# Nine extra matmuls removed, nine weight products read and written in plain order: a decoder layer in split fp32 on one Trainium2 core

## The chip, the cores and the metric

The kernel runs on one NeuronCore of a Trainium2 chip. The metric is device time in microseconds, the median over repeated runs. Beside it stands one profiled execution with its span (first to last instruction) and a trace of every engine. TensorE does matrix products (the profile calls its matmuls PE and its weight loads PEld), VectorE is DVE, ScalarE is ACT, GpSimd is POOL, and SyncE (SP) issues most DMA transfers.

## The reference

One inference step of a one-layer hybrid decoder: a prompt of 256 tokens and 8 samples of 8 tokens share the same weights, so there are T = 320 token columns in all.

```python
xn = rms_norm(x, g_mix)
z = xn @ w_in              # split into b_gate, c_gate, h_conv, q, k, v, gate_c, gate_a
u = c_gate * h_conv
y_conv = (b_gate * short_conv(u, prev, w_conv)) @ w_conv_out
y_attn = window_attention(q, k, v, rel_bias, sinks) @ w_attn_out
merged = sigmoid(gate_c) * y_conv + sigmoid(gate_a) * y_attn
h = x + merged @ w_o
hn = rms_norm(h, g_ffn)
h = h + (silu(hn @ w_gate) * (hn @ w_up)) @ w_down
y = rms_norm(h, g_final)
```

The model width is 2048, the feed-forward width 5632. There are 16 query heads and 4 key/value heads of 64, with a window of 128 keys, a relative-position bias and a learned sink in the softmax. Also returned are the last keys, values and convolution rows of both groups.

## The kernel before, in words

**Features on partitions, tokens on columns.** An activation row is one tile row for 128 features, with 320 columns. A weight product takes a 128x128 block of weights as the stationary operand, streams one row of 320 columns past it and adds into a PSUM bank of 320 of 512 columns.

**Every value is kept as two fp32r parts,** a high part and the low rest. `split_to` (L128 to L130) makes the parts of a weight block: ScalarE copies the block to `whi`, VectorE subtracts that from the block into `wlo`. A product then takes three matmuls for each weight block: high weight by high row, high weight by low row, low weight by high row.

**Products.** `product` (L172) makes two banks of 128 output features over `nk` row chunks. It loads weights four chunks at a time (`load_cols`, 512 KB each through SyncE's queue) and goes through the matmuls in the order that `passes` gives: high and low row for a block at once, the low weight three blocks later. Its matmuls are all recorded on L186. The product of keys and values, `kv_product` (L346), is the same with four banks; its matmuls are on L372. With 16 chunks, a call of `product` is 96 matmuls.

**Plain order and turns.** A row of 320 columns lies in SBUF as five segments of 64 (`row_tiles`, L116): all chunks of segment 0 first, then all of segment 1, with 16 columns of padding after each. So one row is five runs of 64 neighbouring columns, 1,040 columns apart for 16 chunks. The bank is seen as five runs of 64 as well, but these lie one behind the other. `turns` (L101) rearranges such a view so that a matmul takes four columns of the first segment, four of the second and so on, then the next four of the first. Every weight product reads its row and writes its bank in turns. In plain order it would take all 64 columns of a segment before the next one; the bank would then be written from column 0 to 319.

```python
def turns(ap):
    return ap.rearrange("p s (i b) -> p i s b", b=4)
```

**The nudges.** `nudge` (L205 to L207) issues one extra matmul. It reads 320 neighbouring columns from the start of a row tile, uses 128 neighbouring columns of another row as its weights, and writes columns 0 to 319 of a spare PSUM bank that nobody reads. It is called at nine places: once in the product of keys and values before chunk 6 (L353), once before the third query product (L819), three times in the prompt's attention (after the last group of scores, L653, and after each of two groups of value products, L663), twice in the samples' attention (after the scores, L697, and after the value products, L768), and before the first product with `w_up` of each half of the feed-forward part (L1051).

**What sets the order.** The program is written in the order in which TensorE is to run it. The attention and other side work are Python generators. `tick` (L145) takes one step of the generator after every four chunks of a product, so groups of attention matmuls stand between the chunks of the products for q, C, H and B. `issue_after` marks keep the side work behind the last matmul and the last split. The stages run in this order: keys and values; q; C, H and B with attention beside them; the gates with the two output projections (gc, ga, yc, ya); `w_o` (wo); then two halves of the feed-forward part, each with gate and up products in turn (fg, fu) and then the down product (dn).

**Down.** `down` (L974) reads and writes in turns too, with 512 columns per matmul on L997 and 320 on L1005. Two matmuls in each group of 18, on L1001 (dl), stream 512 neighbouring columns into a bank in plain order.

Of the kernel before, what the change touches and what calls it, by code (L numbers as in the profile page):

```python
# [17 lines left out]
T = TP + NB * TS  # L18
# [8 lines left out]
P = 128  # L27
# [25 lines left out]
def hybrid_layer(ctx: ExitStack, tc: tile.TileContext, a: dict, o: list):  # L53
    nc = tc.nc
# [17 lines left out]
    def ps_aux(name):  # L72
        return aux[0].tile([P, 512], F32, tag="aux", name=name)
# [3 lines left out]
    def u(s):  # L77
        uid[0] += 1
        return f"{s}_{uid[0]}"
# [21 lines left out]
    def turns(ap):  # L101

        return ap.rearrange("p s (i b) -> p i s b", b=4)

    def fives(ap):

        return ap.rearrange("p (s j) -> p s j", s=NS)
# [24 lines left out]
    def load_cols(w, k0, n, c0, behind=()):  # L132
# [4 lines left out]
            split_to(hi[:, :n, :], lo[:, :n, :], raw[:, :n, :])  # L137
        return hi, lo

    mark = {}  # L140
    side_work = [None]
    pending = []
    last = {}
# [28 lines left out]
    def product(load, nk, xh, xl, name, tiles=None, loaded=None):  # L172

        ps = [ps_acc(u(name)) for _ in range(2)]
        k0 = 0
        for n in tiles or [min(KT, nk - k) for k in range(0, nk, KT)]:
            hi, lo = load(k0, n)
            if loaded:
                loaded()
            order = [(k, c) for k in range(n) for c in range(2)]  # L180
            if k0 + n == nk:
                order.sort(key=lambda kc: kc[1])
            for k, c, i in passes(order, k0 + n == nk):
                kc = k0 + k
                w, x = ((hi, xh), (hi, xl), (lo, xh))[i]
                last["mm"] = nc.tensor.matmul(  # L186
                    turns(fives(ps[c][:, :T])), w[:, k, c * P:(c + 1) * P], turns(x(kc)),
                    start=(kc == 0 and i == 0), stop=(kc == nk - 1 and i == 2),
                )
            k0 += n  # L190
            while pending:
                with after(last["lo"], last["mm"]):
                    pending.pop(0)()
            tick()
        return ps

    def two_parts(src, tags=("ta", "tb")):
# [3 lines left out]
        nc.scalar.activation(hi, src, AF.Copy)  # L201
        nc.vector.tensor_sub(lo, src, hi.bitcast(F32))
        return hi, lo

    def nudge(rows, weights, n=T):  # L205
        x, w = (bass.AP(r.tensor, r.offset, [list(r.ap[0]), [1, m]]) for r, m in ((rows(0), n), (weights(0), P)))
        nc.tensor.matmul(ps_aux(u("nudge"))[:, :n], w, x, start=True, stop=True)  # L207

    def over_partitions(out, parts):
        for i, x in enumerate(parts):  # L210
# [48 lines left out]
    xh, xl = row_tiles(xp, ("xh_t", "xl_t"), KC, LEAD_X, ("xh", "xl"))  # L259
# [26 lines left out]
    def x_load(i, eng=nc.sync):  # L286
# [11 lines left out]
        out=ident, in_=ident, compare_op=ALU.not_equal, fill=1.0, base=0, pattern=[[-1, P]],  # L298
# [47 lines left out]
    def kv_product(tiles, x_after):  # L346

        ps = [ps_acc(u("kv")) for _ in range(4)]
        k0 = 0
        x_prep(0)  # L350
        for i, n in enumerate(tiles):
            if k0 == 6:
                nudge(xh, xl)  # L353
            hi, lo = load_kv(k0, n)
            if i == 0:
                x_prep(1)
            for b in x_after.get(i, ()):
                x_load(b)
            order = [(k, c) for k in range(n) for c in range(4)]
            if k0 + n == KC:  # L360
                order.sort(key=lambda kc: kc[1])
            seq = passes(order, k0 + n == KC)
            if i == 0:
                seq.sort(key=lambda kcm: kcm[2])
            for k, c, m in seq:
                kc = k0 + k
                if k0 and (k, c, m) == (0, 3 if n > 1 else 1, 0) and k0 + n < KC:
                    for kk in range(tiles[i + 1]):
                        x_prep(k0 + n + kk)
                    tick()  # L370
                w, x = ((hi, xh), (hi, xl), (lo, xh))[m]
                last["mm"] = nc.tensor.matmul(  # L372
                    turns(fives(ps[c][:, :T])), w[:, k, c * P:(c + 1) * P], turns(x(kc)),
                    start=(kc == 0 and m == 0), stop=(kc == KC - 1 and m == 2),
                )
            k0 += n
            if i == 0:
                tick()
        return ps
# [88 lines left out]
    def at_rows(part):  # L468
# [15 lines left out]
        out=sides[:, 0], in_=sides[:, 0], compare_op=ALU.is_ge, fill=0.0, base=-1, pattern=[[-1, WIN]],  # L484
# [158 lines left out]
    def prompt_attention():  # L643
        units = [(j * 2 + par, gp) for j in range(2) for gp in range(2) for par in range(2)]
        bias, sc, sm, turned, pts = {}, {}, {}, {}, {}
        bias[0] = bias_load(*units[0])
        for i in range(len(units) + 3):
            if i < len(units):
                if i + 1 < len(units):
                    bias[i + 1] = bias_load(*units[i + 1])  # L650
                sc[i] = prompt_scores(*units[i], bias.pop(i))
                if i + 1 == len(units):
                    nudge(xh, xl)  # L653
                yield
                sm[i] = prompt_softmax(*units[i], sc[i])
            if 0 <= i - 3 < len(units):
                pts[i - 3] = prompt_sides(i - 3, turned.pop(i - 3))
            yield
            if i >= 4 and i % 4 == 2:
                for n in (i - 5, i - 3):  # L660
                    kv, gp = units[n]
                    prompt_pv(kv // 2, gp, (pts.pop(n - 1), pts.pop(n)))
                nudge(xh, xl)  # L663
            if 0 <= i - 1 < len(units):
                turned[i - 1] = prompt_norm(i - 1, sc.pop(i - 1), *sm.pop(i - 1))
            yield
# [3 lines left out]
    def sample_attention(sm):  # L670
# [10 lines left out]
        for base in range(0, NB, 3):  # L681
            ps = ps_aux(u("pss"))
            n = min(3, NB - base)
            for b in range(base, base + n):
                o0 = (b - base) * W2
                for kv in range(NKV):
                    j, par = kv // 2, kv % 2
                    rows = slice(par * 64, par * 64 + 64)
                    nc.tensor.matmul(
                        ps[kv * 32:(kv + 1) * 32, o0:o0 + W2], qs[rows, j, b, :], kf[rows, b, j, :],  # L690
                        start=True, stop=True,
# [2 lines left out]
                s[:, base:base + n, :], ps[:, 0:n * W2].rearrange("p (b k) -> p b k", b=n),  # L694
                flip(bias_s).unsqueeze(1).to_broadcast([P, n, W2]),
            )
        nudge(xh, xl)  # L697
        yield
        yield

# [49 lines left out]
        for j in range(2):  # L750
            for par in range(2):
# [4 lines left out]
                    start=True, stop=False,  # L756
                )
        for b in range(NB):
            cv = cvs.pop(b)
            for j in range(2):  # L760
                for par in range(2):
# [3 lines left out]
                        cv[:, kv * HD:(kv + 1) * HD], ptw[:, kv, b * 32:(b + 1) * 32],  # L765
                        start=False, stop=(b == NB - 1),
                    )
        nudge(xh, xl)  # L768
        yield
        for j in range(2):  # L770
            src = pos[j][:, 0:256].rearrange("p (b g t) -> p g b t", b=NB, g=GRP)
            o = LEAD_A + j * 4 * at_row
            rows = at_t[:, o:o + 4 * at_row].rearrange("p (g w) -> p g w", g=GRP)[:, :, -2 * JS:]
# [42 lines left out]
    for j in range(2):  # L816
        for gp in range(2):
            if (j, gp) == (1, 0):
                nudge(xh, xl)  # L819
            ps = in_pair(O_Q + (j * 2 + gp) * CW, "q")  # L820
            pending.append(lambda j=j, gp=gp, ps=ps: q_out(j, gp, ps))
    side_work[0] = attention()
# [2 lines left out]
    for cp in range(4):  # L825
        c_sb = []
        ps = in_pair(O_C + cp * CW, "C")
# [4 lines left out]
        ps = in_pair(O_H + cp * CW, "H")  # L832
        conv = []
        for c in range(2):
# [13 lines left out]
            n = UL - 2  # L848
# [10 lines left out]
        ps = in_pair(O_B + cp * CW, "B")  # L859
# [17 lines left out]
    mm = mp_.enter_context(tc.tile_pool(name="mm", bufs=1, side="right"))  # L877
# [9 lines left out]
    for mp in range(8):  # L887
        c0 = mp * CW
        sg = {}
        for nm, off, tag in (("gc", O_GC, "ta"), ("ga", O_GA, "tb")):  # L890
            ps = in_pair(off + c0, nm)
# [5 lines left out]
        ps = product(  # L897
            lambda k0, n: load_cols(w_co, k0, n, c0), 8,
            cv_h, cv_l, "yc",
        )  # L900
# [126 lines left out]
    for half in range(2):  # L1027
# [4 lines left out]
        for fpair in range(nf // 2):  # L1032
            c0 = (f0 + fpair * 2) * P
            psg = product(
                lambda k0, n: load_cols(w_g, k0, n, c0), KC,
                hh, hl, "fg",
            )
            if half == 0 and fpair == 0:
                pss = ps_aux("pss2")
                over_partitions(pss[:, :T], two_parts(hacc, ("tc", "td")))  # L1040
                rstd_of(pss[:, :T], [P, T], "r2", hp, out=rb2)
            gs = []
            for c in range(2):
                t, t2 = tmp("ta", "gs")[:, :T], tmp("tb", "sg")[:, :T]
                nc.vector.tensor_mul(t, psg[c][:, :T], rb2)
                last["sig"] = nc.scalar.activation(t2, t, AF.Sigmoid)
                nc.vector.tensor_mul(t, t, t2)
                nc.vector.tensor_mul(t, t, rb2)
                gs.append(t)
            if fpair == 0:  # L1050
                nudge(hh, hl)  # L1051
            psu = product(
                lambda k0, n: load_cols(w_u, k0, n, c0), KC,
                hh, hl, "fu",
            )
            for c in range(2):
                nc.vector.tensor_mul(gs[c], psu[c][:, :T], gs[c])
                f = fpair * 2 + c
                (first, rest), row = parts_of(gs[c]), a_move(f)
                nc.scalar.activation(row[:, :, JR:JT], rest, AF.Copy)  # L1060
                last["hi"] = nc.scalar.activation(row[:, :, 0:JR], first, AF.Copy)
                nc.vector.tensor_sub(row[:, :, JT:], rest, row[:, :, JR:JT].bitcast(F32))
                last["lo"] = nc.vector.tensor_sub(placed(a_low(f)), first, row[:, :, 0:JR].bitcast(F32))
                if half == 1:
                    nc.scalar.activation(a_first(f), gs[c][:, 0:P], AF.Copy)
# [258 lines left out]
```

## Time and profile before

| | us |
|---|---|
| median of 3 runs (1593.12 to 1593.64) | 1593.38 |
| profiled execution | 1593.85 |
| its span | 1592.1 |
| PE busy | 1583.2 |
| weight loads busy (beside PE) | 1547.1 |
| DVE busy | 890.9 |
| ACT busy | 645.9 |

The profiled execution is 0.47 us over the median. Its span is 1.75 us short of its own time; that is what lies around the span. TensorE's clock was granted at 0.998 over the span. A matmul's row in the trace gives its start and its duration; the duration counts the way through the array as well (301 ns for 320 columns), and the next matmul starts before it has ended. What a matmul costs in a dense stream is thus the distance from its start to the next start, not the duration.

### The profile page before, as it was taken

How to read it: one execution, taken by the hardware profiler on the slowest of the kernel's cores; microseconds unless marked ns; L12 is line 12 of the kernel's file. 1: busy time of each engine (PE TensorE's matmuls, PEld its weight loads, DVE VectorE, ACT ScalarE, POOL GpSimd, SP SyncE). 2: the span in 40 equal slices, each digit the busy share in tenths (PEclk: the TensorE clock that was granted, in tenths of full speed). 3: DMA queues.
4: the chain of work that ended last, by engine and by line, in shares of the span. 5: the costliest groups of instructions: out<-in, count | busy, mean ns of one | idle time of the engine just before them, and what ended most of it. 6: DMA issues, size and time to landing. Idle time of an engine off the chain costs nothing.

```text
span 1592.1 us, 26453 instructions
## 1 busy us (share of the span) xinstructions
PE 1583.2 (99%) x10899; PEld 1547.1 (97%) x10899; DVE 890.9 (56%) x1314; ACT 645.9 (41%) x917; POOL 133.2 (8%) x213
## 2 busy tenths in 40 slices
PE   9999999999999999999999999999999999999998
PEld 9999999999999999999999999998888999999887
DVE  7879765445555445556555555553444455555556
ACT  7554443333333333344333333333333334444443
POOL 1414332000000003320000000000000000000021
PEclk9999999999999999999999999999999999999999
DMA  7757566544455544455554545555555454445663
GB/s 271 207 182 218 171 211 203 166 154 155 157 159 159 159 156 155 155 158 159 157 154 155 159 158 159 159 156 161 155 155 157 157 159 158 156 155 157 190 180 131
DMA packets 77648, 266.06 MB, mean 167 GB/s; under 512 B 9832, under 2 KB 13112, under 8 KB 77400
## 3 DMA queue, kind: packets, MB, share of 16 engines
q1 hardware_dynamic: 71736, 249.99, 50.2%
q0 software_dynamic: 5360, 13.84, 3.0%
q8 instruction: 85, 1.39, 0.4%
q10 hardware_dynamic: 432, 0.56, 0.1%
q14 instruction: 35, 0.29, 0.1%
HBM read 257.27 MB, written 9.04 MB: 167 GB/s over the span
## 4 chain that ended last, share of the span: by engine, by line
PE 99%; DMA 0%; DVE 0%; ACT 0%; issue 0%; SPq 0%; DVEq 0%
PE fu L186 19%; PE fg L186 19%; PE dn L997 9%; PE wo L186 7%; PE gc L186 7%; PE ga L186 7%; PE dn L1005 6%; PE C L186 3%; PE B L186 3%; PE H L186 3%; PE q L186 3%; PE ya L186 3%; PE yc L186 3%; PE dl L1001 2%; PE kv L372 2%; PE dn L1162 1%
## 5 line engine op out<-in xcount | busy, mean ns | idle before, releaser
L130 DVE TENSOR_TENSOR wlo<-wraw,whi 128x1024 fp32r<-128x1024 f32 (+1 forms) x460 | 563.1, 1225 | 564.5 <-ACT whi L129 453.4
L129 ACT ACTIVATE whi<-wraw 128x1024 fp32r<-128x1024 f32 (+1 forms) x460 | 485.5, 1056 | 722.0 <-PE fu L186 129.5
L186 PE MATMUL fu<-hh_t,whi 128*128 128x320 f32 x704 | 205.0, 301 | 0.0
L186 PE MATMUL fu<-hl_t,whi 128*128 128x320 f32 x704 | 205.0, 301 | 0.0
L186 PE MATMUL fg<-hh_t,whi 128*128 128x320 f32 x704 | 205.0, 301 | 0.0
L186 PE MATMUL fg<-hl_t,whi 128*128 128x320 f32 x704 | 205.0, 301 | 0.0
L186 PE MATMUL fu<-hh_t,wlo 128*128 128x320 f32 x704 | 158.8, 301 | 0.0
L186 PE MATMUL fg<-hh_t,wlo 128*128 128x320 f32 x704 | 158.8, 301 | 0.0
L997 PE MATMUL dn<-a_t,whi 128*128 128x512 f32 x640 | 155.2, 382 | 0.0
L186 PEld LDWEIGHTS fu<-hh_t,whi 128*128 128x128 f32 x704 | 131.7, 187 | 0.0
L186 PEld LDWEIGHTS fu<-hl_t,whi 128*128 128x128 f32 x704 | 131.7, 187 | 0.0
L186 PEld LDWEIGHTS fg<-hh_t,whi 128*128 128x128 f32 x704 | 131.7, 187 | 0.0
L186 PEld LDWEIGHTS fg<-hl_t,whi 128*128 128x128 f32 x704 | 131.7, 187 | 0.0
L997 PEld LDWEIGHTS dn<-a_t,whi 128*128 128x128 f32 x640 | 115.4, 187 | 16.5 <-issue 1.2
L186 PEld LDWEIGHTS fg<-hh_t,wlo 128*128 128x128 f32 x704 | 116.1, 187 | 0.0
L186 PEld LDWEIGHTS fu<-hh_t,wlo 128*128 128x128 f32 x704 | 116.1, 187 | 0.0
L1005 PEld LDWEIGHTS dn<-a_t,wlo 128*128 128x128 f32 x640 | 97.7, 188 | 6.9
L1005 PE MATMUL dn<-a_t,wlo 128*128 128x320 f32 x640 | 103.4, 301 | 0.0
L186 PE MATMUL gc<-xh_t,whi 128*128 128x320 f32 x256 | 74.5, 301 | 0.0
L186 PE MATMUL gc<-xl_t,whi 128*128 128x320 f32 x256 | 74.5, 301 | 0.0
L186 PE MATMUL ga<-xh_t,whi 128*128 128x320 f32 x256 | 74.5, 301 | 0.0
L186 PE MATMUL ga<-xl_t,whi 128*128 128x320 f32 x256 | 74.5, 301 | 0.0
(317 smaller groups left out, 2695.7 us busy)
## 6 DMA issues: line engine op xcount, KB each, us to landing
wraw<-in_w_in_dram SPq DMA_DIRECT2D x128, 512.0 KB, 3.9
wraw<-in_w_gate_dram SPq DMA_DIRECT2D x88, 512.0 KB, 3.8
wraw<-in_w_up_dram SPq DMA_DIRECT2D x88, 512.0 KB, 3.7
wraw<-in_w_down_dram SPq DMA_DIRECT2D x88, 512.0 KB, 3.7
wraw<-in_w_o_dram SPq DMA_DIRECT2D x32, 512.0 KB, 3.8
wraw<-in_w_conv_out_dram SPq DMA_DIRECT2D x16, 512.0 KB, 3.6
wraw<-in_w_attn_out_dram SPq DMA_DIRECT2D x16, 512.0 KB, 3.7
wraw<-in_w_kv_dram SPq DMA_DIRECT2D x6, 512.0 KB, 7.5
```

What stands on the lines that cost most here:

```text
L129: last["hi"] = nc.scalar.activation(hi, src, AF.Copy)
L130: last["lo"] = nc.vector.tensor_sub(lo, src, hi.bitcast(F32))
L186: last["mm"] = nc.tensor.matmul(turns(fives(ps[c][:, :T])), w[:, k, c * P:(c + 1) * P], turns(x(kc)), start=(kc == 0 and i == 0), stop=(kc ...
L372: last["mm"] = nc.tensor.matmul(turns(fives(ps[c][:, :T])), w[:, k, c * P:(c + 1) * P], turns(x(kc)), start=(kc == 0 and m == 0), stop=(kc ...
L997: nc.tensor.matmul(turns(placed(ps[c])), parts[k][0][:, cs], turns(a_move(k)), start=k == 0, stop=False)
L1001: nc.tensor.matmul(low, a_low(k), parts[k][0], start=k == 0, stop=k == nf - 1 and c0 < E0)
L1005: last["mm"] = nc.tensor.matmul(turns(placed(ps[c])[:, :, 0:JT]), parts[k][1][:, cs], turns(a_move(k)[:, :, 0:JT]), start=False, stop=k == ...
L1162: nc.tensor.matmul(turns(placed(ps[c])[:, :, JR:]), held[k][0][:, cs], turns(a_move(k)[:, :, JR:]), start=k == 0, stop=k == nf - 1,)
```

## The change

`nudge` no longer issues anything: it sets a flag. A new helper `weigh` issues the matmuls of `product` and `kv_product`; if the flag is set, it clears it and leaves out `turns` for this one matmul, in what it reads and in what it writes. All other products run in turns as before. The nine calls stand where they stood.

```diff
+    plain = [False]
+
+    def weigh(out, w, x, **kw):
+        walk = (lambda ap: ap) if plain[0] else turns
+        plain[0] = False
+        last["mm"] = nc.tensor.matmul(walk(fives(out)), w, walk(x), **kw)
+
+    def nudge():
+        plain[0] = True
...
-                last["mm"] = nc.tensor.matmul(
-                    turns(fives(ps[c][:, :T])), w[:, k, c * P:(c + 1) * P], turns(x(kc)),
+                weigh(
+                    ps[c][:, :T], w[:, k, c * P:(c + 1) * P], x(kc),
                     start=(kc == 0 and i == 0), stop=(kc == nk - 1 and i == 2),
                 )
...
-    def nudge(rows, weights, n=T):
-        x, w = (bass.AP(r.tensor, r.offset, [list(r.ap[0]), [1, m]]) for r, m in ((rows(0), n), (weights(0), P)))
-        nc.tensor.matmul(ps_aux(u("nudge"))[:, :n], w, x, start=True, stop=True)
...
-                nudge(xh, xl)
+                nudge()
```

The same two edits are made in `kv_product`, and the calls with `hh, hl` lose their arguments too. The program has nine matmuls and nine weight loads fewer, and uses nine spare banks fewer from the ring of four (`ps_aux`).

More of the change, by code (lines that the diff above doesn't have):

```diff
@@ L371, in kv_product @@
                 w, x = ((hi, xh), (hi, xl), (lo, xh))[m]
-                last["mm"] = nc.tensor.matmul(
-                    turns(fives(ps[c][:, :T])), w[:, k, c * P:(c + 1) * P], turns(x(kc)),
+                weigh(
+                    ps[c][:, :T], w[:, k, c * P:(c + 1) * P], x(kc),
                     start=(kc == 0 and m == 0), stop=(kc == KC - 1 and m == 2),
@@ L652, in prompt_attention @@
                 if i + 1 == len(units):
-                    nudge(xh, xl)
+                    nudge()
                 yield
@@ L662, in prompt_attention @@
                     prompt_pv(kv // 2, gp, (pts.pop(n - 1), pts.pop(n)))
-                nudge(xh, xl)
+                nudge()
             if 0 <= i - 1 < len(units):
@@ L696, in sample_attention @@
             )
-        nudge(xh, xl)
+        nudge()
         yield
@@ L767, in sample_attention @@
                     )
-        nudge(xh, xl)
+        nudge()
         yield
@@ L818, in hybrid_layer @@
             if (j, gp) == (1, 0):
-                nudge(xh, xl)
+                nudge()
             ps = in_pair(O_Q + (j * 2 + gp) * CW, "q")
@@ L1050, in hybrid_layer @@
             if fpair == 0:
-                nudge(hh, hl)
+                nudge()
             psu = product(
```

## The prediction

> **What bounds the kernel now.** I read the page first: how busy each engine is, the granted clock, the chain that ended last. Then the list of waits of TensorE.
>
> ```profile
> PE 1583.2 (99%) x10899; PEld 1547.1 (97%) x10899; DVE 890.9 (56%) x1314; ACT 645.9 (41%) x917; POOL 133.2 (8%) x213
> ...
> PEclk9999999999999999999999999999999999999999
> ...
> PE 99%; DMA 0%; DVE 0%; ACT 0%; issue 0%; SPq 0%; DVEq 0%
> ```
>
> ```profile
> PE wm L305 <- PEq L1304: 0.8, 1, 0.8
> PE kv L372 <- ACT whi L129: 0.6, 1, 0.6
> ```
>
> TensorE is the chain from end to end, at its full clock, and waits twice in the whole span, both times before 7.5 us. So the time is a sum of distances from one matmul's start to the next, and only these distances can change. I therefore asked the windows view for the number of product matmuls in stretches that I had cut, in the timeline, at their ends. The first number of a row is the stretch in us, the (x...) behind it is the count.
>
> ```profile
> 91.50:101.73 10.23, 10.23 (x72) 10.15 (x72) 1.00 0.52 162
> 102.45:112.55 10.10, 10.10 (x72) 10.01 (x72) 1.00 0.73 224
> 170.53:197.50 26.97, 26.97 (x192) 26.80 (x192) 1.00 0.56 166
> 256.61:710.22 453.61, 453.61 (x3240) 453.53 (x3240) 1.00 0.51 160
> 710.67:1073.56 362.89, 362.89 (x2592) 362.81 (x2592) 1.00 0.50 157
> 1274.53:1476.14 201.61, 201.61 (x1441) 201.53 (x1440) 1.00 0.50 157
> ```
>
> ```profile
> 7.20:15.83 8.63, 8.63 (x60) 8.55 (x60) 1.00 1.02 392
> ```
>
> Two paces of the same matmul show. 453.61 / 3240 is 0.1400 us, and so is 362.89 / 2592. But 10.23 / 72 is 0.1421, and 8.63 / 60 (with one longer first step) is 0.144. Call them the even and the uneven pace; they differ by 0.0021 us, or 1.5%. The uneven one holds over the first 60 matmuls and over the 72 behind one group of attention scores. Nearly everything else runs at the even pace. What ends the uneven pace can be seen at the first nudge, at 15.84, and the nudge's own price as well:
>
> ```profile
> 15.27 0.73 PE L372 MATMUL kv<-xh_t,wlo 128*128 128x320 f32 x4
> 15.84 0.31 PE L207 MATMUL nudge<-xh_t,xl_t 128*128 128x320 f32 x1
> 15.99 0.30 PE L372 MATMUL kv<-xh_t,whi 128*128 128x320 f32 x1
> 16.13 0.30 PE L372 MATMUL kv<-xl_t,whi 128*128 128x320 f32 x1
> 16.27 0.31 PE L372 MATMUL kv<-xh_t,whi 128*128 128x320 f32 x1
> 16.42 0.30 PE L372 MATMUL kv<-xl_t,whi 128*128 128x320 f32 x1
> 16.56 0.30 PE L372 MATMUL kv<-xh_t,whi 128*128 128x320 f32 x1
> ```
>
> The nudge takes 0.15, one or two steps behind it are long by up to 0.01, and the pace is even from there. A matched pair, both groups of scores entered from the even pace, shows that the nudge matters. At 91.50 products in turns follow the scores at once, and the pace is uneven for 72 of them. At 170.38 a nudge stands between, and 26.97 us hold 192 matmuls, 0.1405 with the settling at the front:
>
> ```profile
> 91.39 0.28 PE L565 MATMUL ps<-k,at_t 128*128 128x256 f32 x1
> 91.50 0.30 PE L186 MATMUL C<-xh_t,whi 128*128 128x320 f32 x1
> 91.64 0.30 PE L186 MATMUL C<-xl_t,whi 128*128 128x320 f32 x1
> ```
>
> ```profile
> 170.26 0.28 PE L565 MATMUL ps<-k,at_t 128*128 128x256 f32 x1
> 170.38 0.31 PE L207 MATMUL nudge<-xh_t,xl_t 128*128 128x320 f32 x1
> 170.53 0.31 PE L186 MATMUL B<-xh_t,whi 128*128 128x320 f32 x1
> 170.68 0.30 PE L186 MATMUL B<-xl_t,whi 128*128 128x320 f32 x1
> ```
>
> So the question is not what nine matmuls cost but whether a weight product in plain order does the nudge's work.
>
> **The change part by part.** *What is removed:* nine nudges. Beside 15.84 to 15.99 and 170.38 to 170.53, seven more stand in the timeline: the last of the attention part, the one behind the sum over partitions, and the last one are:
>
> ```profile
> 256.36 0.41 PE L207 MATMUL nudge<-xh_t,xl_t 128*128 128x320 f32 x1
> 256.61 0.31 PE L186 MATMUL B<-xh_t,whi 128*128 128x320 f32 x1
> ```
>
> ```profile
> 710.23 0.46 PE L211 MATMUL pss<-part,ones_r 128*128 128x320 f32 x2
> 710.53 0.31 PE L207 MATMUL nudge<-hh_t,hl_t 128*128 128x320 f32 x1
> 710.67 0.31 PE L186 MATMUL fu<-hh_t,whi 128*128 128x320 f32 x1
> ```
>
> ```profile
> 1273.82 0.72 PE L186 MATMUL fg<-hh_t,wlo 128*128 128x320 f32 x4
> 1274.38 0.31 PE L207 MATMUL nudge<-hh_t,hl_t 128*128 128x320 f32 x1
> 1274.53 0.31 PE L186 MATMUL fu<-hh_t,whi 128*128 128x320 f32 x1
> ```
>
> ```profile
> L207 PE MATMUL nudge<-xh_t,xl_t x7: 309/414/414, 15.8 to 256.4; 128*128 128x320 f32 x7
> ```
>
> The median of 414 ns says that four of the seven are of the long kind, like the one at 256.36, which stands behind the samples' value products and is 0.25 from the next start. The short ones shown take 0.14 to 0.15. The long kind pays for the switch from narrow tiles to the full array: whichever 320-column matmul comes first will pay that 0.11, and after the change it is the plain product. So each place saves one normal step, the 0.140 us of the windows: 9 x 0.140 = 1.26 us. All of it is on the path, since TensorE has no idle time to hide it in.
>
> *What is added:* nothing is issued; nine products that were there change their order. The price is bounded by what the trace has of plain order. The two sums over partitions at 710.23 read and write 320 columns in plain order: 0.30 for two, 0.150 each, or 0.01 over the even pace. The nudge at 15.84 is the same. Behind it two steps are long, 0.14 to 0.15. All of this is paid today around every nudge and would be paid around every plain product, so it cancels; I take it as zero. If the settling vanished with the nudge, another 9 x 0.02 = 0.2 us would go; if it came twice, 0.2 would come back. If the switch's 0.11 went at the four long places too, 0.4 more would go. The bounds of the main case are thus 1.06 and 1.9 saved.
>
> The Trainium skill has a rule that speaks about this order. "Advanced Engine Details and Errata", section "PSUM Cachelines", says that any non-contiguous pattern in PSUM slows a matmul significantly, and wants every two neighbouring elements to stay together. Read as written, plain order would be the quicker one, so the nine plain products would gain rather than pay, some 0.1 us by my estimate if the 0.01 above had its sign turned. The trace disagrees with it as a general rule: 0.150 in plain order against 0.140 in turns of four.
>
> *What is moved:* the plain product needs its row and its high weights, where the nudge needed only a row. If these were late, up to 0.15 us per place of cover would be gone. At the first place ScalarE's split had ended at 14.54, 1.45 us early, and the list of waits has no wait for a split after 7.5 us:
>
> ```profile
> 13.50 1.04 ACT L129 ACTIVATE whi<-wraw 128x1024 fp32r<-128x1024 f32 x1
> ```
>
> I price it at nothing. No DMA moves and no queue is passed. The ring of four spare banks has nine takers fewer, so whoever takes one looks back to an older user: no new wait. VectorE and ScalarE have 56% and 41%, and what they gain or lose is not on the path.
>
> *Sum.* Profiled execution 1593.85 - 1.26 = 1592.59; the median stands 0.47 below the profiled one, so 1593.38 - 1.26 = **1592.1 us**. That is 0.08% of the time; about 0.2%, 3.2 us, is what a measurement of this kernel can tell from no change. I expect a gain that is real in the trace and too small for a verdict.
>
> **The rivals.** *One long stretch falls to the uneven pace.* A plain product is not quite a nudge: it reads five runs with jumps between, where the nudge reads one run, and six of the nine add into a bank that the next matmul uses again, where the nudge wrote a bank of its own. If one of the last three places is left uneven, it stays so to the next different matmul, and the price is the count by 0.0021: 3240 x 0.0021 = 6.8 us from 256.61, 2592 x 0.0021 = 5.4 from 710.67, 1441 x 0.0021 = 3.0 from 1274.53. The time would be 1598.9, 1597.5 or 1595.1. For it: the pace depends on little things, since scores alone leave it uneven at 91.50 and even at 102.45. Against it: wherever 320 columns in plain order went through, nine nudges out of nine, the pace behind was even. It decides from 1.26 / 0.0021 = 600 uneven matmuls on; below that the change still gains.
>
> *Plain products do not work at all.* Then all nine places are left as they would be without nudges. The three long stretches cost 15.2; the early places add at most (256.61 - 15.99) / 0.140 = 1,719 matmuls or 3.6 us, and the time is up to 1592.1 + 18.8 = 1610.9. That is the worst case, as some places were even before their nudge (from 1273.82 to 1274.38 four matmuls take 0.56, 0.140 each) and may stay even without it. For it: only that nobody has a plain product in this trace. Against it: the two properties that could matter, a plain read and a plain write, are both there.
>
> *Small places only.* The pace is lost at one or more of the six early places. The one at 170.38 is good for its 192 matmuls, 0.4 us, and all six for the 3.6 just bounded: 1592.5 to 1595.7, most likely below 1594.
>
> *It does nothing.* Plain products bring a step of their own as long as the nudge, say by waiting for the bank that the product before has just written: 1593.4. Against it: the second of the two sums at 710.23 adds into the bank of the first and takes no longer.
>
> **How the numbers follow.** All places hold: 0.75. Small places only: 0.05. Nothing: 0.04. One long stretch: 0.11, of it 0.03 for the last (1595.1, within 0.2%), and 0.08 for the others. None works: 0.04. A further 0.01 is for a gain over 0.2% by something not in this trace. Slower by over 0.2% is then 0.08 + 0.04 = 0.12, faster 0.01, same 0.75 + 0.05 + 0.04 + 0.03 = 0.87. The main case alone spans 1593.38 - 1.9 to 1593.38 - 1.06, and with 0.3 for the spread of the runs 1591.2 to 1592.6. To leave out no more than 2 in 10 the range takes in "nothing" and "small places": up to 1594.3. All of the long stretches stay out.
>
> **What would show it right or wrong.** Right: L207 is gone, PE has 10890 matmuls, nine of them on the lines of the products last about 10 ns longer than their neighbours, the windows from about 257, 711 and 1275 us hold their 3240, 2592 and 1440 matmuls at 0.140, and the span is near 1590.8. A step wrong: the distance from a plain product to its successor is over 0.16 where no narrow tile stands ahead, or the first matmuls behind it do not settle within ten. The prediction falls if one of these three windows is 3 us or more longer for its count.

## The result and the profile after

| | before | after |
|---|---|---|
| median, us | 1593.32 (6 runs, 1593.12 to 1593.64) | 1599.70 (6 runs, 1599.29 to 1600.30) |
| ratio to before | | 1.0040 (95% interval 1.0027 to 1.0053) |
| profiled execution, us | 1593.85 | 1599.29 |
| its span, us | 1592.1 | 1597.6 |

The change makes the kernel 6.4 us slower, 0.4%, where 1.3 us less was forecast. The page after shows the nine matmuls gone, TensorE still the whole chain, and no other engine's busy time changed by 1 us. In the list of waits one line is left, at the program's start:

```profile
span 1597.6 us, 26435 instructions
...
PE 1589.4 (99%) x10890; PEld 1553.6 (97%) x10890; DVE 890.4 (56%) x1314; ACT 646.3 (40%) x917; POOL 134.1 (8%) x213
...
PE 99%; DVE 0%; issue 0%; DVEq 0%; ACT 0%
```

```profile
PE wm L311 <- PEq L1310: 0.8, 1, 0.8
```

So fewer matmuls took 6 us more of TensorE's time without waiting for anything: the pace is what changed. To compare kernels I cut the same windows in all of them and let the view count the product matmuls in each. It also counts those that only overlap an edge of the window, so a count is some two above the division: 440 us hold 3,145 at the even pace of 0.140 us, and 32 us hold 230 or 231 at the even pace and 227 or 228 at the uneven one. Before, then after:

```profile
172.00:196.00 24.00, 24.00 (x173) 24.00 (x172) 1.00 0.57 172
218.00:250.00 32.00, 32.00 (x231) 32.00 (x230) 1.00 0.52 159
260.00:700.00 440.00, 440.00 (x3145) 440.00 (x3144) 1.00 0.51 159
720.00:1060.00 340.00, 340.00 (x2431) 340.00 (x2430) 1.00 0.50 157
1290.00:1470.00 180.00, 180.00 (x1288) 180.00 (x1288) 1.00 0.50 156
```

```profile
172.00:196.00 24.00, 24.00 (x171) 24.00 (x170) 1.00 0.58 172
218.00:250.00 32.00, 32.00 (x231) 32.00 (x230) 1.00 0.60 181
260.00:700.00 440.00, 440.00 (x3096) 440.00 (x3095) 1.00 0.51 157
720.00:1060.00 340.00, 340.00 (x2431) 340.00 (x2430) 1.00 0.51 157
1290.00:1470.00 180.00, 180.00 (x1288) 180.00 (x1287) 1.00 0.51 158
```

After, the third row has 49 matmuls fewer in the same time: 440 / 3096 is 0.1421, the uneven pace. The first row (172 to 196, behind the last group of prompt scores) is uneven as well, with 171 for 173. The others are even. The whole long stretch has its 3,240 matmuls in

```profile
255.38:716.03 460.65, 460.65 (x3240) 460.57 (x3239) 1.00 0.51 157
```

which is 0.1422 each, 0.0022 over the even pace. The sum closes: 3240 x 0.0022 = 7.1, plus 192 x 0.0022 = 0.4 behind the scores, less 9 x 0.140 = 1.26, gives 6.3 of the 6.4 measured. (The two profiled executions differ by 5.4 only: the one before reached the first of the nine places at 15.84 us, the one after at 15.05. This start differs from one execution to the next, up to 16.00 in a later run, so two single executions can stand about 1 us apart for that alone.) The timeline of the changed kernel shows how the long stretch begins. The product at 255.13 is the one in plain order:

```profile
255.13 0.41 PE L145 MATMUL B<-xh_t,whi 128*128 128x320 f32 x1
255.38 0.31 PE L145 MATMUL B<-xl_t,whi 128*128 128x320 f32 x1
255.52 0.31 PE L145 MATMUL B<-xh_t,whi 128*128 128x320 f32 x1
255.67 0.30 PE L145 MATMUL B<-xl_t,whi 128*128 128x320 f32 x1
255.81 0.30 PE L145 MATMUL B<-xh_t,whi 128*128 128x320 f32 x1
255.95 0.30 PE L145 MATMUL B<-xl_t,whi 128*128 128x320 f32 x1
256.09 0.30 PE L145 MATMUL B<-xh_t,whi 128*128 128x320 f32 x1
```

It pays its 0.25 for the switch from narrow tiles, as the nudge did. The next steps differ by no more than 0.01 us from the even ones, but the stream never settles.

The places are numbered here in the order in which they run: 1 keys and values, 2 third query product, 3 first value products, 4 last prompt scores, 5 second value products, 6 samples' scores, 7 samples' value products, 8 and 9 the two halves of the feed-forward part.

### The profile page after: what moved, and what is told of

It reads as the page before. It is cut to its first block, busy times and chain, and to the rows that moved or that the text cites. A ratio compares the mean times of both kernels' runs of the same rounds, so it can differ in the third digit from the quotient of the medians.

```text
span 1597.6 us, 26435 instructions
## 1 busy us (share of the span) xinstructions
PE 1589.4 (99%) x10890; PEld 1553.6 (97%) x10890; DVE 890.4 (56%) x1314; ACT 646.3 (40%) x917; POOL 134.1 (8%) x213
## 4 chain that ended last, share of the span: by engine, by line
PE 99%; DVE 0%; issue 0%; DVEq 0%; ACT 0%
PE fg L145 19%; PE fu L145 19%; PE dn L1003 9%; PE wo L145 7%; PE ga L145 7%; PE gc L145 7%; PE dn L1011 6%; PE B L145 3%; PE yc L145 3%; PE ya L145 3%; PE H L145 3%; PE C L145 3%; PE q L145 3%; PE dl L1007 2%; PE kv L145 2%; PE dn L1168 1%
## 5 line engine op out<-in xcount | busy, mean ns | idle before, releaser
L145 PE MATMUL wo<-m_h,whi 128*128 128x320 f32 x256 | 75.6, 304 | 0.0
```

Of the source, the lines that this page charges most:

```text
L145: last["mm"] = nc.tensor.matmul(walk(fives(out)), w, walk(x), **kw)
```

## The experiments

Of each edit only the lines that matter are printed; `w0` is the nudge's block of weights. Three of the kernels (e5, e10, e14) add a matmul into a bank that is used afterwards; that changes what they compute, and they serve for timing alone.

**First round: what a place needs.** Four kernels: no nudge and no plain product at all; the extra matmul kept but reading as the plain product does; kept but wholly in turns; and the changed kernel with one nudge put back at place 7.

```diff
 # e1_none: before, with
 def nudge(rows, weights, n=T):
+    return
```

> No nudge and no plain product at any of the nine places; every weight product in turns. Theory A (the settling needs a matmul in plain order, and a plain product that reads five runs is a weaker one than a nudge that reads one run): the first place is uneven up to the query products, and the stretch behind the samples' value products (3240 products) is uneven as in the changed kernel, about 1599 us. Rival C (the pace behind a disturbance is a matter of phase, and it was the plain product itself that left this stretch uneven): the 3240 products run at 0.140 us and the time is near 1592.5 us. If all long stretches are uneven, about 1607 to 1610 us.

```diff
 # e2_fiveread: before, with
-    nc.tensor.matmul(ps_aux(u("nudge"))[:, :n], w, x, start=True, stop=True)
+    nc.tensor.matmul(fives(ps_aux(u("nudge"))[:, :n]), w, rows(0), start=True, stop=True)
```

> The nine extra matmuls of the kernel before, with one thing changed: they read five runs of 64 columns (a row as the plain product reads it) where the nudge reads one run of 320. They still write a spare bank in plain order. Theory A (the broken read is what makes the plain product fail): the 3240 products behind the samples' value products are uneven, 1593.4 + 6.8 = about 1600 us. Rival B (it fails since it adds into the bank that the next matmul uses): even, 1593.4 us. Rival C (phase alone): any of the two, and other places may change too.

```diff
 # e3_turned: before, with
+    nc.tensor.matmul(turns(fives(ps_aux(u("nudge"))[:, :n])), w, turns(rows(0)), start=True, stop=True)
```

> The nine extra matmuls read and write in turns, like a normal product, into the spare bank. Theory A and the kernel's own idea (plain order is what settles the pace): the extra matmul does nothing, all places go as without nudges plus 1.26 us. Rival B (an extra matmul into another bank is what counts): even everywhere, 1593.4 us. Rival C: places change one by one, not all in the same direction.

```diff
 # e4_spo_extra: after, at place 7 only (extra = the old nudge)
-        nudge()
+        extra(xh, xl)
```

> The changed kernel with one nudge put back as an extra matmul, at the place behind the samples' value products; the other eight stay plain products. All theories that put the loss at this one place: 1599.7 - 3240 x 0.0021 + 0.14 = about 1593 us, and with the other eight matmuls saved 1592.3 to 1592.8. If the loss lay elsewhere as well (the wait for weights, the ring of spare banks), it stays above 1595.

Measured: 1600.16, 1599.25 and 1593.69 us, a single execution of each (before beside them: 1593.56, 15 runs), and for the last 1592.69 (11 runs, 1592.27 to 1593.07; ratio 0.9995, 0.9986 to 1.0004). The windows of the first, second and third kernel, in this order:

```profile
172.00:196.00 24.00, 24.00 (x171) 24.00 (x170) 1.00 0.57 174
218.00:250.00 32.00, 32.00 (x228) 32.00 (x227) 1.00 0.58 176
260.00:700.00 440.00, 440.00 (x3096) 440.00 (x3095) 1.00 0.49 157
720.00:1060.00 340.00, 340.00 (x2430) 340.00 (x2429) 1.00 0.49 157
```

```profile
260.00:700.00 440.00, 440.00 (x3145) 440.00 (x3144) 1.00 0.50 159
720.00:1060.00 340.00, 340.00 (x2393) 340.00 (x2392) 1.00 0.49 155
```

```profile
218.00:250.00 32.00, 32.00 (x227) 32.00 (x226) 1.00 0.56 170
260.00:700.00 440.00, 440.00 (x3145) 440.00 (x3144) 1.00 0.50 159
```

Without any nudge, places 4, 6 and 7 come out uneven. The other six are even all the same, place 8 with its 2,592 matmuls and place 1 among them (102 products in the 14 us from 17). With an extra matmul that reads five runs, places 6 and 7 are even, place 4 is uneven, and place 8 is *lost*. With one in turns, places 4, 7 and 8 are even and only place 6 is uneven. So theory A, that the broken read makes the plain product weak, has fallen at the very place that it was made for, and "plain order settles the pace" is no rule either. The first kernel's time came near theory A's, but its place 1 did not; rival C (phase alone) missed place 7 there, and allowed for what came in the second and third without saying which. The fourth kernel went as expected: one matmul put back at place 7 takes 7.0 us off the changed kernel, so the loss is there and nowhere else but place 4.

**Second round: what is different about place 7.** From here on, place 4 has no plain product, and place 7 alone is varied (the last of the four has the old nudge there). Taking the plain product out at place 4 is thus a second difference from the changed kernel in every run of this and the next two rounds; what it does by itself is measured only in the last round.

```diff
 # e5_dup: at place 7, ahead of the first product, which stays in turns
+        nc.tensor.matmul(turns(fives(out)), w, turns(x), **kw)
```

> The changed kernel with the plain product taken back to turns at two places: behind the last group of scores (nothing instead), and behind the samples' value products, where the first weight product is issued a second time, in turns, into its own bank (it is added twice there, so a part of one product of B counts double). Rival B (the bank decides): an extra matmul into the bank that the next one uses helps nothing; the 3240 products stay uneven, about 1599.3 us. Theory D (one more step of any kind in front of the stream decides at this place; read order and bank do not): even, about 1592.3 us. Both theories: the 192 products behind the last scores are even, 0.4 us less than in the changed kernel.

```diff
 # e6_alt: at place 7, no extra matmul, order of the first four products
+            seq[1:3] = seq[2:0:-1]
```

> As the run before, but without any extra matmul behind the samples' value products: the first four products there, in turns, take the two banks in alternation (first bank, second, first, second) where the order was first, first, second, second. Rival B: even, 3240 products at 0.140, about 1592.1 us with no extra matmul at all. Theory D: still a stream of the same steps, so uneven, about 1599.2 us.

```diff
 # e7_plain2: at place 7, plain order for two products
-        plain[0] = False
+        plain[0] = plain[0] == "twice"
```

> As the two runs before, but behind the samples' value products the first two products are in plain order, not one. If plain order works and one product was too little (theory A in its weak form): even, about 1592.1 us. Theory D gives no sign in advance; rival B: both go into the same bank, so uneven, about 1599.2 us.

```diff
 # e8_best: place 4 without a plain product, place 7 with the old nudge
-                if i + 1 == len(units):
-                    nudge()
...
-        nudge()
+        extra(xh, xl)
```

> The changed kernel with the two places mended that the trace shows uneven: the extra matmul behind the samples' value products put back, and nothing behind the last group of scores (products in turns there). All theories in which a place's outcome is fixed by the matmuls around it: 1592.69 - 192 x 0.0021 = 1592.3 us, below the kernel before by about 1.2. If the outcome were drawn anew in each execution, some runs would stand several us higher.

Measured: 1599.64, 1598.91 and 1592.12 us in single executions, and 1592.27 (11 runs, 1591.96 to 1592.87; ratio 0.9993, 0.9984 to 1.0002). The stretch behind place 7 holds 3,096, 3,096, 3,145 and 3,145. The rows of the first three:

```profile
260.00:700.00 440.00, 440.00 (x3096) 440.00 (x3095) 1.00 0.49 157
```

```profile
260.00:700.00 440.00, 440.00 (x3096) 440.00 (x3095) 1.00 0.50 157
```

```profile
260.00:700.00 440.00, 440.00 (x3145) 440.00 (x3145) 1.00 0.50 160
```

Rival B said that alternating banks would settle it: they do not. Theory D said that one more step of any kind would: a step in turns does not. With two plain products it is even. Place 4, left alone, came out even in all four, which is worth 0.4 us by the windows (192 x 0.0022).

**Third round: bank or operands, one plain product or two.** The turned extra matmul of the last round had the next product's bank and operands; the one that had worked at this place had neither.

```diff
 # e9_own_ops: the extra matmul of e5 into a spare bank
-            nc.tensor.matmul(turns(fives(out)), w, turns(x), **kw)
+            nc.tensor.matmul(turns(fives(ps_aux(u("spare"))[:, :T])), w, turns(x), start=True, stop=True)
 # e10_own_bank: the extra matmul of e5 with the nudge's weights and row
+            nc.tensor.matmul(turns(fives(out)), w0, turns(xh(0)), **kw)
 # e11_second: plain order for the second product alone
-        walk = (lambda ap: ap) if plain[0] else turns
+        walk = (lambda ap: ap) if plain[0] is True else turns
```

> The run with the doubled product, with one thing changed: the extra matmul in turns, with the same weights and the same row as the first product, now writes a spare bank that nobody reads. Theory E (an extra matmul settles the place only if its bank is not the one that follows): even, about 1592.3 us. Theory F (what settles it is that the nudge reads another row and other weights than the product that follows): uneven, about 1599.5 us.

> The extra matmul in turns with the nudge's weights and row (a block of the low row as weights, row 0), but added into the bank of the product that follows, so that this product of B is changed. Theory E: uneven, about 1599.5 us. Theory F: even, about 1592.3 us. If this run and the run before come out alike, neither property decides alone.

> No extra matmul; behind the samples' value products the first product is in turns and the second one in plain order (the run with two plain products had both). If one plain product is too little of a push: uneven, about 1599.2 us. If its distance from the narrow matmuls matters: even, about 1592.1 us.

The kernel with two plain products was also timed:

> The kernel with two plain products behind the samples' value products and none behind the last scores, no extra matmul anywhere, timed this time. If the outcome of each place is fixed by the matmuls around it: 1592.1 us in every run, 1.2 below the kernel before (0.08%) and 0.1 to 0.2 below the version with one extra matmul. If it is drawn anew: single runs near 1599.

Measured: 1599.64, 1599.39 and 1592.36 us in single executions, and 1592.27 us (11 runs, 1591.71 to 1592.99; ratio 0.9992, 0.9983 to 1.0001). A turned extra matmul failed in the spare bank with the product's operands and in the product's bank with the nudge's, so neither theory E nor F holds; with a plain product in second position the place is even. That left one contradiction: in the first round a turned extra matmul had worked at place 7.

**Fourth round: the same place, another past.**

```diff
 # e13_plain_own_ops: extra matmul at place 7 in plain order, own operands, spare bank
+            nc.tensor.matmul(fives(ps_aux(u("spare"))[:, :T]), w, x, start=True, stop=True)
 # e14_plain_own_bank: in plain order, the nudge's operands, the product's bank
+            nc.tensor.matmul(fives(out), w0, xh(0), **kw)
 # e15_turned_spare: in turns, the nudge's operands, spare bank, as in e3
+            nc.tensor.matmul(turns(fives(ps_aux(u("spare"))[:, :T])), w0, turns(xh(0)), start=True, stop=True)
 # e16_turned_spare_un: e15, and nothing at place 6
-        nudge()
```

> One extra matmul in plain order behind the samples' value products (five runs read, plain write) into a spare bank, with the weights and the row of the product that follows. Theory G (in plain order an extra matmul settles this place whatever its bank and operands; one plain product does not since it is itself the first step and a turned one follows too early): even, about 1592.3 us. Theory E' (the spare bank is what makes the nudge work): even too. Theory F' (the other row and weights are): uneven, 1599.5 us.

> The same extra matmul in plain order with the nudge's weights and row, added into the bank of the product that follows, so that this product of B is changed. Theory G: even, about 1592.3 us. Theory E': uneven, 1599.5 us. Theory F': even.

> One extra matmul in turns at this place, with the nudge's weights, row and spare bank, exactly as in the kernel where all nine extra matmuls were in turns and this place was even. The difference is the pace ahead of the narrow matmuls: uneven there, even here. Theory H (the pace at the entry takes part in what comes out): uneven, 1599.5 us. If it comes out even, the entry does not matter, and spare bank and other operands work together.

> The run before with nothing behind the samples' scores, so that the pace ahead of the value products is uneven (264 products, 0.6 us more). Theory H: the 3240 products are even, about 1592.9 us. Without an influence of the entry they come out as in the run before.

Measured: 1592.09, 1592.79, 1599.70 and 1591.96 us, a single execution of each (before: 1593.52). With the extra matmul in plain order the place is even, with the spare bank and with the product's own, with the product's operands and with the nudge's, as theory G had it (but see the last round). In turns, with the nudge's bank and operands, it is uneven. And in the last kernel, where nothing at place 7 is different and one product at place 6 is back in turns, it is even. (The 0.7 us between the first two is their start: they reach place 1 at 15.24 and 16.00.) The windows of the third kernel, then of the fourth:

```profile
218.00:250.00 32.00, 32.00 (x230) 32.00 (x229) 1.00 0.58 178
260.00:700.00 440.00, 440.00 (x3096) 440.00 (x3095) 1.00 0.50 157
```

```profile
218.00:250.00 32.00, 32.00 (x231) 32.00 (x230) 1.00 0.53 164
260.00:700.00 440.00, 440.00 (x3145) 440.00 (x3144) 1.00 0.50 160
```

Theory H has fallen in its words: I expected place 6 to come out uneven and the pace ahead of place 7 to matter, but the pace there is even in both (32 us hold 230 and 231). The same matmuls, met at the same pace, come out differently. Something that the pace does not show, and that the edit at place 6 altered, decides at place 7: call it the phase. I take it to be carried along the stream. An alignment with another engine or with the transfers would look the same in these two runs and was not tested.

**Last round: the change's own plain product with another past.**

```diff
 # e17_no_scores: after, without the plain product at place 4
-                if i + 1 == len(units):
-                    nudge()
 # e18_no_scores_pss: e17, also without the one at place 6
-        nudge()
```

> The changed kernel without the plain product behind the last prompt scores; all else as changed, so one plain product stands behind the samples' value products, where the changed kernel is uneven. Theory I (what a place comes out as hangs on the matmuls there and on a phase that is carried over from the places ahead): the 192 products behind the scores are even (0.4 us less), and the 3240 may come out either way, though nothing within 80 us ahead of them is altered. Theory K (one plain product as the first step is too little at this place, whatever went before): uneven, 1599.7 - 0.4 = 1599.3 us.

> The run before, also without the plain product behind the samples' scores, which was the edit that turned the outcome for an extra matmul in turns. Theory I: the 3240 products are even with the very plain product that fails in the changed kernel, about 1592.0 us; Theory K: uneven, about 1599.3 us. Either way the 264 products behind the samples' scores are even, as in the last run.

Measured: 1592.19 us (10 runs, 1591.79 to 1592.50; ratio 0.9991, 0.9982 to 1.0000) and 1599.14 us (5 runs, 1598.64 to 1599.64; ratio 1.0037, 1.0023 to 1.0051). Windows of the first, then of the second:

```profile
172.00:196.00 24.00, 24.00 (x174) 24.00 (x173) 1.00 0.55 170
218.00:250.00 32.00, 32.00 (x231) 32.00 (x230) 1.00 0.55 169
260.00:700.00 440.00, 440.00 (x3145) 440.00 (x3144) 1.00 0.50 160
```

```profile
218.00:250.00 32.00, 32.00 (x231) 32.00 (x230) 1.00 0.61 186
260.00:700.00 440.00, 440.00 (x3096) 440.00 (x3096) 1.00 0.49 158
```

The first of the two is the changed kernel with one plain product taken back to turns some 85 us ahead of place 7. At place 7 it has the same single plain product, and there the stream begins like this:

```profile
254.86 0.42 PE L145 MATMUL B<-xh_t,whi 128*128 128x320 f32 x1
255.11 0.31 PE L145 MATMUL B<-xl_t,whi 128*128 128x320 f32 x1
255.26 0.31 PE L145 MATMUL B<-xh_t,whi 128*128 128x320 f32 x1
255.41 0.31 PE L145 MATMUL B<-xl_t,whi 128*128 128x320 f32 x1
255.55 0.31 PE L145 MATMUL B<-xh_t,whi 128*128 128x320 f32 x1
255.70 0.30 PE L145 MATMUL B<-xl_t,whi 128*128 128x320 f32 x1
255.84 0.30 PE L145 MATMUL B<-xh_t,whi 128*128 128x320 f32 x1
```

Behind the first step there are four steps of about 0.15 and then even ones, where the changed kernel had two longer steps and never settled. (The trace file keeps starts to the nanosecond; there the four are 151, 148, 146 and 150 ns, and the two are 144 and 147.) Theory K (one plain product as the first step is too little here) has fallen with this run. The second run went against what was expected under theory I: with the plain product at place 6 gone too, the stretch was to be even at 1592.0, and it is uneven at 1599.14. What is left of theory I is its general form, that what a place comes out as hangs on its matmuls and on something settled at the places ahead of it; it does not say which way. A second pair agrees. At place 4, with scores and then products in turns in both, the kernel without nudges holds 171 in its 24 us and e17 holds 174; the difference between them lies at the places before.

The first run also changes how the rounds before it are to be read. With place 4 free of its plain product, one plain product at place 7 is enough, so the even outcomes with two plain products and with extra plain matmuls (e7, e12, e13, e14) do not show that anything had to be added at place 7. In the timelines e13 and e14 begin like e17: 0.25, four longer steps, then even. The change at place 4 explains them as well. Against the changed kernel itself, with its own past, only the old nudge was tried at place 7 (e4).

The phase may show in a view after all. The pace ahead of place 7 is the same in the changed kernel, e17 and e18, but the recorded durations there are not (240 to 249 us, `--source`, in this order):

```profile
L145 PE MATMUL H<-xh_t,wlo x24: 301/301/301, 239.7 to 248.5; 128*128 128x320 f32 x24
L145 PE MATMUL H<-xh_t,wlo x23: 302/302/302, 239.9 to 248.3; 128*128 128x320 f32 x23
L145 PE MATMUL H<-xh_t,wlo x22: 301/301/301, 239.9 to 247.9; 128*128 128x320 f32 x22
```

The two that show 301 ns come out uneven, the one with 302 even. For the pair with the extra matmul in turns it is the other way round: 302 in e15 (uneven), 301 in e16 (even). So in both comparisons the stream arrives in a different condition. One nanosecond is the step in which the trace records, and that this difference is the cause is not shown.

## Why the prediction was wrong

**The bound, the paces, the place of the gain: right.** TensorE stayed the whole chain. The two paces and their prices came out as read: 0.0021 was used and 0.0022 measured. Nine steps were saved: the changed kernel less its loss, 1599.70 - 7.1 - 0.4 = 1592.2, and e17, with one plain product fewer, measured 1592.19 where 1592.1 was forecast.

**The step that failed** is the one that carried the forecast: "wherever 320 columns in plain order went through, nine nudges out of nine, the pace behind was even", from which a plain product was given the nudge's work at every place. It was given to the case in which all places hold (0.75); what happened is the first rival, one long stretch at the uneven pace, priced at 1598.9 with a chance of 0.11 in all, and place 4 with its 0.4 us beside it. Nine out of nine was no evidence about the cause, because there was no place without a nudge among the nine. The runs showed the control that was missing: without any nudge six of the nine places are even anyway (e1). The prediction had seen this at one place (four matmuls in 0.56 us ahead of the last nudge) and used it only for its worst case. At place 7 the plain product left 3,240 matmuls at 0.1422 us in the changed kernel, 7.1 us, and at 0.140 in e17. And the nine outcomes are not nine trials: an edit at place 4 or 6 alone turns the outcome at place 7.

**"All of this is paid today and would be paid around every plain product, so it cancels": right in size, but not what mattered.** The long steps behind a nudge were priced at some 0.02 us a place; in e17 the four behind place 7 take 0.59 us (255.11 to 255.70) where even ones take 0.56. What costs is the pace behind them, and the number of long steps doesn't tell it: e17 is even behind four, the changed kernel uneven behind two, and e3 even at place 7 with none.

**The matched pair (91.50 and 170.38) was read as what a nudge does.** It compares two places, not one place with and without. At the first of them nothing stands in any of these kernels, and its 72 products take 10.24 us in the kernel before (91.50 to 101.74) and 10.09 in e2 (90.89 to 100.98). At the second, which is place 4, the kernel without nudges is uneven with nothing there, but e17 is even with nothing, and the changed kernel is uneven with its plain product. The prediction took the need of a place as fixed.

**The bank and the five runs,** named in the first rival as reasons, do not decide by themselves. The plain product of e17 reads five runs and adds into its own bank, and the stretch behind it is even. Whether they take part in the changed kernel, with its own past, was not tried.

**Weights in time, ring of spare banks, other engines: right.** No wait for them came.

**The order itself:** the plain product at place 2 took 0.15 to its successor, as forecast from the sums over partitions. The rule that any non-contiguous pattern in PSUM slows a matmul significantly (the Trainium skill, "Advanced Engine Details and Errata", section "PSUM Cachelines") finds no support here either, as the step in turns is 0.14:

```profile
59.45 0.31 PE L145 MATMUL q<-xh_t,whi 128*128 128x320 f32 x1
59.60 0.30 PE L145 MATMUL q<-xl_t,whi 128*128 128x320 f32 x1
59.74 0.30 PE L145 MATMUL q<-xh_t,whi 128*128 128x320 f32 x1
```

**What stays open.** The phase was inferred from outcomes: apart from the one nanosecond above no view used here shows it, and these runs do not tell what part of the machine holds it. There is no rule from the matmuls at a place to what comes out; one kernel's list of even and uneven places doesn't carry over to the next edit. Why the plain product at place 4 leaves the stream uneven, and why taking out the one at place 6 as well loses place 7 again, was not tried further.

## What to carry to other kernels

In a dense matmul stream, count matmuls per fixed window before and after any edit, also behind edits far ahead of it: 49 missing in 3,145 is a loss that no wait and no busy share shows. A remedy that was seen to work nine times says little until one place is run without it. Where a pace depends on what came before, mend the places by trial, one at a time, with all else left as it is, and keep the cheapest that the windows show even: here that was the change itself less one plain product, 1592.19 us against 1593.62 before, 0.1%, with an interval that just reaches no change (0.9982 to 1.0000).

## What was not expected of the hardware

No pace between the two was seen. In the 20 traces the 440 us window held 3,145 matmuls or 3,095 to 3,096, never anything else. The uneven pace is a pattern, too: in the changed kernel nine steps take 1.28 us (169.30 to 170.58), where nine even ones take 1.26. In the trace file the steps behind place 7 repeat 142, 142, 143, 142, 141, 144, 141, 142, 143 ns, where the even ones are 140 each.

```profile
169.30 0.30 PE L145 MATMUL B<-xl_t,whi 128*128 128x320 f32 x1
...
170.58 0.30 PE L145 MATMUL B<-xl_t,whi 128*128 128x320 f32 x1
```

What comes out at place 7 was the same in every execution of a program, though it hangs on so little and though the start differs between executions: the 6 runs of the changed kernel lie within 1.0 us, the 10 and 11 runs of e17 and of the kernel with two plain products within 0.7 and 1.3, and none of them shows the 7 us of the other outcome.
